# First layer of a hybrid decoder: another spacing of the recurrence's matmuls, and convolutions that scale their copy in SBUF

## The chip, the cores and the metric

The kernel runs on one core of a Trainium2 chip. The metric is the device time of one execution in microseconds (us). Three runs of the kernel before took 2169.34, 2174.07 and 2175.66 us (median 2174.07). The profile that is read below is of one further execution, which took 2167.99 us; its span from the first to the last instruction is 2166.2 us.

## The reference, cut to what matters

A sequence of 1040 tokens (16 meta tokens and 1024 tokens of input) passes two layers of width 1024. The first is a gated DeltaNet: q, k and v come from one projection, a causal convolution over 4 tokens and a SiLU; then a linear recurrence over chunks, per head. The second layer (latent attention) is not touched by the change.

```python
qkv, z, b, a = split(h @ w_in)
qkv = silu(causal_depthwise_conv(qkv, conv_w))        # 4 taps
...
def step(state, xs):                                  # one chunk of one head
    v_new = u_c - w_c @ state
    o_c   = qd_c @ state + a_c @ v_new
    state = state * gl_c + kd_c.T @ v_new
```

## The kernel before, in words

**Work of the first layer.** The 16 value heads are handled as 8 groups of 2 (one query/key head each). For each group, columns of the input projection are computed 128 at a time, transposed: 128 channels on the partitions, 1040 tokens along the free axis, in three pieces of 400, 384 and 256 tokens, each in its own PSUM bank (tile `pt`, tag `proj`, 3 banks in all, so one column of 128 channels fills them). The products are made as three fp32r matmuls (high and low halves), 72 matmuls for a column. A column is a query, a key, one of two gates `z` or one of two values `vT`.

**Emptying a column.** For queries, keys and values `conv_ev` does, for each of the three pieces: copy the last 3 tokens of the piece before out of its bank into the front of an SBUF tile `xpad` (L423), copy the piece itself behind them (L424), scale the piece by the fourth tap into the output tile (L427, on ScalarE, read from the bank `pt`), add the other three taps on VectorE (L429, read from `xpad`), and a SiLU by tanh (L431, L432). `xpad` has 3 buffers. The value column's output `vT` is one tile of 1040 tokens with one buffer: the second value column of a group can be written only when the first one's transposes (L632) have read it. The banks of a column are free for the next column when L423, L424 and L427 have read them.

**The recurrence.** `rec_chunk(g, c)` does chunk c (128 tokens) of group g: `ksp`, the key's product with the state `S` (PE); `r` on VectorE (L739); `xps`, the product of the inverse `U` with `r` (PE); its copy `x` (ScalarE, L747); `sps`, the state's update product (PE); the new state (VectorE, L758); `oq`, the output's products (PE); and the output `o` (L772, L773) with its sum of squares (L783). The state of a chunk is needed by `ksp` of the next. `kd` (L727, GpSimd, one buffer) is made at the chunk's start and read by `sps`.

**What sets the order.** `rec_chunk` is a generator. The loop over groups and chunks takes 5 steps of it per chunk, and after each step some steps of side work (`fills(g)`: the projections, convolutions, the triangular inverse of the next group, all of it independent of this chunk), 77 steps per group over 45 slots, so 1.7 per slot. So the place of a `yield` says how much side work stands between two parts of a chunk. This order of the program text gives each instruction its priority only: a planner orders each engine's queue when the kernel is built. It lets an instruction go ahead of one of higher priority that, by the planner's own estimate of durations, isn't ready. The parts under `with first():` (the two state steps on VectorE and the copy `x`) have priority over everything. On the chip each queue runs in that fixed order; an instruction that waits holds up all behind it.

**A lone bank.** Transposes of k, q, v (`tok_stats`, `v_tokens`) and of the gated outputs (`out_`) share one PSUM bank (tag `tr`). The recurrence's products share four banks (tag `tp`).

Of the kernel before, what the change touches and what calls it, by code (L numbers as in the profile page):

```python
# [9 lines left out]
AF = mybir.ActivationFunctionType  # L10
# [35 lines left out]
def build(nc, tc, A, out, dbg=None):  # L46
    dbg = dbg or {}
    act, dve, pool, pe, sp = nc.scalar, nc.vector, nc.gpsimd, nc.tensor, nc.sync
# [13 lines left out]
    def mm(out_, l, r, start, stop):  # L62
        pe.matmul(out_, l, r, start=start, stop=stop)  # L63
# [108 lines left out]
    with contextlib.ExitStack() as g_es:  # L172
# [170 lines left out]
        @contextlib.contextmanager  # L343
        def first():

            tc.cur_priority -= 4000
            yield
            tc.cur_priority += 4000
# [64 lines left out]
        def conv_ev(ct, dst, new):  # L413

            wc = lambda i: wcv[:, i * 32 + ct:i * 32 + ct + 1]

            def ev(pts, i, n0, n):
                xp = gp.tile([P, 403], F32, name="xpad", bufs=3)
                if i == 0:
                    pool.memset(xp[:, 0:3], 0.0)  # L420
                else:
                    pn = NCH[i - 1][1]
                    act.copy(xp[:, 0:3], pts[i - 1][:, pn - 3:pn])  # L423
                act.copy(xp[:, 3:3 + n], pts[i][:, :n])  # L424
                o = new(i)
                dst.append(o)
                act.activation(o, pts[i][:, :n], AF.Copy, scale=wc(3))  # L427
                for j in (2, 1, 0):
                    dve.scalar_tensor_tensor(o, xp[:, j:j + n], wc(j), o, op0=ALU.mult, op1=ALU.add)  # L429
                t = gp.tile([P, 400], F32, name="tanh", bufs=3)  # L430
                act.activation(t[:, :n], o, AF.Tanh)  # L431
                dve.scalar_tensor_tensor(o, t[:, :n], 1.0, o, op0=ALU.add, op1=ALU.mult)  # L432
            return ev
# [4 lines left out]
        def chunk(src, c):  # L438

            i = [c in cs for _, _, cs in NCH].index(True)  # L440
            t0, n = TOK[c]
            return src[i][:, t0 - NCH[i][0]:t0 - NCH[i][0] + n]
# [277 lines left out]
        def rec_chunk(g, c):  # L720
            s = st[g]
            t0, n = TOK[c]
            kT, qT, AT = s["k"], s["q"], s["AT"][c]
            U = s["U"].pop(c)
            hd = lambda x, h: x[:, c, 2 * g + h:2 * g + h + 1]
            kd = gp.tile([P, 2, 128], F32, name="kd", bufs=1)
            pool.tensor_tensor(kd, s["ktok"][c].unsqueeze(1).broadcast_to([P, 2, 128]),  # L727
                               s["kds"][:, c].unsqueeze(2).broadcast_to([P, 2, 128]), op=ALU.mult)
            if c == 0:
                rr = [s["v"][0, h] for h in range(2)]  # L730
            else:
                S = s["S"]
                ksp = ps.tile([P, 2, 128], F32, name="ksp", tag="tp", bufs=4)
                mm(ksp, chunk(kT, c), S, True, True)
                yield
                r = gp.tile([P, 2, 128], F32, name="r", bufs=1)
                with first():
                    for h in range(2):
                        dve.scalar_tensor_tensor(r[:, h], ksp[:, h], hd(egc, h), s["v"][c, h], op0=ALU.mult, op1=ALU.subtract)  # L739
                rr = [r[:, h] for h in range(2)]  # L740
            xps = ps.tile([P, 2, 128], F32, name="xps", tag="tp", bufs=4)
            for h in range(2):
                mm(xps[:, h], U[:, h], rr[h], True, True)
            yield
            x = gp.tile([P, 2, 128], F32, name="x", bufs=1)
            with first():
                act.copy(x, xps)  # L747
            sps = ps.tile([P, 2, 128], F32, name="sps", tag="tp", bufs=4)
            for h in range(2):
                mm(sps[:, h], kd[:, h], x[:, h], True, True)  # L750
            yield
            Sn = gp.tile([P, 2, 128], F32, name="S", bufs=2)
            if c == 0:
                act.copy(Sn, sps)
            else:
                with first():
                    for h in range(2):
                        dve.scalar_tensor_tensor(Sn[:, h], S[:, h], egl[:, c, 2 * g + h:2 * g + h + 1], sps[:, h],  # L758
                                                 op0=ALU.mult, op1=ALU.subtract)
            s["S"] = Sn  # L760
            oq = ps.tile([P, 2, 2, 128], F32, name="oq", tag="tp", bufs=4)
            for h in range(2):
                mm(oq[:, 1, h], AT[:, h], x[:, h], True, True)
            if c:
                mm(oq[:, 0], chunk(qT, c), S, True, True)
            yield
            o = gp.tile([P, 2, 128], F32, name="o", bufs=8)
            if c == 0:
                act.copy(o, oq[:, 1])
            else:  # L770
                for h in range(2):
                    act.activation(o[:, h], oq[:, 0, h], AF.Copy, scale=hd(egc, h))  # L772
                dve.tensor_tensor(o, o, oq[:, 1], op=ALU.subtract)  # L773
            ci = [c in cs for _, _, cs in NCH].index(True)
            i = NCH[ci][2].index(c)
            if i == 0:
                s["oss"] = gp.tile([P, 4, 2], F32, name="oss", bufs=3)
                s["o"] = []
                if c == 0:
                    pool.memset(s["oss"], 1.0)  # L780
            for h in range(2):
                jk = gp.tile([P, 128], F32, name="jk", bufs=1)
                act.activation(jk[:n], o[:n, h], AF.Square, accum_out=s["oss"][:n, i, h:h + 1])  # L783
            s["o"].append(o)
            if c == NCH[ci][2][-1]:
                gate(g, ci, s["o"], s["oss"])
# [126 lines left out]
        for g in range(8):  # L913
# [5 lines left out]
            for c in range(9):  # L919
                tg = iter(())  # L920
                if c == 0 and g < 2:
                    tg = t_half(g, 0)
                elif c == 1:
                    t_load(g, 1)
                elif c == 3:
                    tg = t_half(g, 1)
                elif c == 7 and 0 < g < 7 or c == 8 and g == 0:
                    st[g + 1]["U"] = {}
                    t_load(g + 1, 0)
                elif c == 8 and g < 7:  # L930
                    tg = t_half(g + 1, 0)
                tg = shifted(tg, TPRIO)
                rg = shifted(rec_chunk(g, c), RPRIO)
                for _ in range(STAGES):
                    next(tg, None)
                    next(rg, None)
                    stages += 1
                    while done * 9 * STAGES < stages * nfill:
                        next(fl_, None)
                        tick()  # L940
                        done += 1
                assert next(tg, None) is None and next(rg, None) is None
# [6 lines left out]
    def bank(tag, bufs):  # L949
        return ps.tile([P, 512], F32, name="b_" + tag, tag=tag, bufs=bufs)  # L950
# [129 lines left out]
    with w1_es:  # L1080
# [62 lines left out]
        for tis in GROUPS:  # L1143
# [3 lines left out]
            pts = [bank("a", 4) for _ in tis]  # L1147
# [481 lines left out]
    with tp_(name="w2", bufs=1) as w2p:  # L1629
# [34 lines left out]
        for tis in groups2:  # L1664
            first = tis[0] == 1
            pts = w2pts if first else [[bank(*(("tr", 3) if ti in (3, 6) else ("a", 4))) for _ in range(2)] for ti in tis]
# [42 lines left out]
```

## Time and profile before

| | us |
|---|---|
| median of three runs | 2174.07 |
| profiled execution | 2167.99 |
| its span | 2166.2 |
| TensorE busy | 2045.9 (94%) |
| VectorE busy | 1359.4 (63%) |
| ScalarE busy | 1102.3 (51%) |
| GpSimd busy | 740.5 (34%) |
| mean granted TensorE clock | 0.980 of full |

The first layer's recurrence lies from about 175 to 1055 us of the span; the groups follow each other about every 118 us. A line of the profile names source line, engine, operation and tiles (out<-in), then its time; a bracket at its end gives how long the engine stood idle before it and what ended the idle time. "Busy" of TensorE counts instructions at whatever clock was granted. The granted clock has two levels, 1.2 and 2.4 GHz; a mean of 0.89 over a stretch is a mixture of both.

### The profile page before, as it was taken

What the parts mean: (1) busy time and instruction counts of PE and PEld (TensorE: products, weight loads), DVE (VectorE), ACT (ScalarE), POOL (GpSimd) and SP (SyncE); (2) the same over time, 40 slices, a digit from 0 to 9 for tenths busy, and PEclk for the clock granted to TensorE, in tenths of its full rate; (3) what the DMA queues carried; (4) which work ended last, traced back from release to release, by engine and by line L of the source; (5) the groups of instructions that cost most, each with busy time, mean ns of one, the idle gap of its engine ahead of it and who ended that gap; (6) DMA issues with size and microseconds to landing.
All of it is one profiled execution on the core that took longest, in us unless ns stands there. A gap on an engine that the chain in (4) does not pass through costs nothing.

```text
span 2166.2 us, 38604 instructions
## 1 busy us (share of the span) xinstructions
PE 2045.9 (94%) x13407; PEld 1823.8 (84%) x13407; DVE 1359.4 (63%) x3135; ACT 1102.3 (51%) x3323; POOL 740.5 (34%) x1718
## 2 busy tenths in 40 slices
PE   7899888999999898999899999999999999999998
PEld 6898778989899898987677898888998999987886
DVE  6585866685858585765446543436777877885422
ACT  5655455656464746555334454335665656664311
POOL 4343535455464545441301482301304132010111
PEclk9999999999999999999899999999999999999999
DMA  3123122222221212124445431221111111124431
GB/s 119 51 55 75 40 61 67 56 66 53 61 62 43 75 51 74 47 66 110 138 116 174 141 91 61 88 95 44 40 50 40 49 35 50 40 81 163 160 100 41
DMA packets 237420, 164.02 MB, mean 76 GB/s; under 512 B 78476, under 2 KB 217304, under 8 KB 237224
## 3 DMA queue, kind: packets, MB, share of 16 engines
q1 hardware_dynamic: 225472, 140.12, 23.0%
q0 software_dynamic: 4128, 13.15, 1.6%
q10 hardware_dynamic: 7624, 8.27, 1.2%
q8 instruction: 106, 1.74, 0.3%
q14 instruction: 90, 0.74, 0.1%
HBM read 121.27 MB, written 40.19 MB: 75 GB/s over the span
## 4 chain that ended last, share of the span: by engine, by line
PE 71%; DVE 15%; DMA 4%; ACT 4%; issue 3%; POOL 2%; SPq 1%; DVEq 0%; ACTq 0%; POOLq 0%
PE b_a L63 27%; PE pt L63 17%; PE b_tr L63 8%; PE b_pv L63 5%; PE b_tr L1493 3%; DVE pr L577 2%; PE oq L63 2%; DVE pr L600 1%; DVE tu L579 1%; PE sps L63 1%; DVE pr L593 1%; DVE MT L549 1%; PE xps L63 1%; DVE AT L550 1%; PE ksp L63 1%
## 5 line engine op out<-in xcount | busy, mean ns | idle before, releaser
L63 PE MATMUL pt<-hsh,whi 128*128 128x400 f32 (+2 forms) x1128 | 372.7, 333 | 14.5 <-ACT xpad L423 10.6
L63 PE MATMUL pt<-hsl,whi 128*128 128x400 f32 (+2 forms) x1128 | 369.6, 328 | 0.0
L63 PE MATMUL pt<-hsh,wlo 128*128 128x400 f32 (+2 forms) x1128 | 368.0, 328 | 1.1 <-POOL wlo L392 1.1
L392 POOL TENSOR_TENSOR wlo<-raw,whi 128x256 fp32r<-128x256 f32 x188 | 154.2, 825 | 252.1 <-ACT whi L391 242.5
L63 PEld LDWEIGHTS pt<-hsh,whi 128*128 128x128 f32 x1128 | 214.5, 190 | 19.6 <-ACT xpad L423 12.4
L63 PEld LDWEIGHTS pt<-hsh,wlo 128*128 128x128 f32 x1128 | 213.3, 190 | 2.9 <-POOL wlo L392 1.8
L63 PEld LDWEIGHTS pt<-hsl,whi 128*128 128x128 f32 x1128 | 214.3, 190 | 1.4
L1469 POOL COPY p<-p 128x32 f32<-128x32 f32 x128 | 28.9, 226 | 334.1 <-ACT p L1466 313.9
L1466 ACT ACTIVATE p<-b_a,mx 128x256 f32<-128x256 f32 (+4 forms) x224 | 120.8, 546 | 41.1 <-DVE mx L1458 17.7
L60 DVE TENSOR_TENSOR ptl<-b_tr,pth 128x512 fp32r<-128x512 f32 x192 | 104.6, 550 | 24.0 <-ACT pth L59 21.8
L59 ACT CAST pth<-b_tr 128x512 fp32r<-128x512 f32 x192 | 91.5, 487 | 51.8 <-PE b_tr L1493 50.3
L1451 DVE TENSOR_REDUCE mx<-b_a 128x1 f32<-128x256 f32 (+4 forms) x224 | 110.9, 504 | 9.0 <-PE b_a L63 5.7
L59 ACT CAST gh<-graw 128x512 fp32r<-128x512 f32 (+1 forms) x86 | 51.0, 602 | 124.8 <-PE b_a L63 83.8
L429 DVE SCALAR_TENSOR_TENSOR vT<-xpad,wcv,vT 128x256 f32<-128x256 f32 (+2 forms) x144 | 92.4, 684 | 30.0 <-ACT xpad L423 25.5
L60 DVE TENSOR_TENSOR gl<-graw,gh 128x512 fp32r<-128x512 f32 x82 | 55.7, 688 | 81.3 <-ACT gh L59 80.0
L391 ACT CAST whi<-raw 128x256 fp32r<-128x256 f32 x188 | 75.5, 404 | 57.0 <-PE pt L63 27.2
L1493 PE MATMUL b_tr<-cm,p 128*128 128x128 f32 x576 | 93.7, 274 | 1.3 <-ACT wt L1373 0.7
L63 PE MATMUL b_a<-hsh,gh 128*128 128x512 f32 (+1 forms) x224 | 87.9, 399 | 5.9 <-ACT ojunk L978 4.2
L1292 DVE SCALAR_TENSOR_TENSOR wlo<-raw,vecs,whi 128x128 fp32r<-128x128 f32 x128 | 45.1, 383 | 72.6 <-ACT whi L1291 70.7
L727 POOL TENSOR_TENSOR kd<-ktok,kds 128x256 f32<-128x256 f32 x72 | 60.7, 843 | 83.9 <-PE sps L63 83.7
L63 PE MATMUL b_a<-hsl,gh 128*128 128x512 f32 (+1 forms) x224 | 87.7, 399 | 0.2
L63 PE MATMUL b_a<-ckth,qah 128*128 128x256 f32 (+4 forms) x224 | 81.8, 365 | 3.9 <-ACT p L1466 3.9
(610 smaller groups left out, 6055.4 us busy)
## 6 DMA issues: line engine op xcount, KB each, us to landing
raw<-in_gdn_w_in SPq DMA_DIRECT2D x192, 128.0 KB, 2.2
graw<-g1scr SPq DMA_DIRECT2D x52, 256.0 KB, 3.3
raw<-in_mla_w_in SPq DMA_DIRECT2D x64, 128.0 KB, 2.2
zscr<-z SPq DMA_DIRECT2D x16, 512.0 KB, 2.8
zh<-zscr SPq DMA_DIRECT2D x32, 256.0 KB, 3.5
g2scr<-g2t POOLq DMA_DIRECT2D x32, 256.0 KB, 3.4
graw<-g2scr SPq DMA_DIRECT2D x30, 256.0 KB, 3.0
wraw<-in_mla_w_out SPq DMA_DIRECT2D x13, 512.0 KB, 4.8
```

The costliest lines, as they stand in the source:

```text
L59: act.copy(hi, src)
L60: dve.tensor_tensor(lo, src, f(hi), op=ALU.subtract)
L63: pe.matmul(out_, l, r, start=start, stop=stop)
L391: act.copy(hi, raw)
L392: pool.tensor_tensor(lo, raw, f(hi), op=ALU.subtract)
L429: dve.scalar_tensor_tensor(o, xp[:, j:j + n], wc(j), o, op0=ALU.mult, op1=ALU.add)
L577: dve.tensor_tensor(prv, T[:, :, 0:i, 0:i].rearrange("p h j c -> p h c j"), bd[:, :, 0:i, i].unsqueeze(2).broadcast_to([65, 2, i, i]), op= ...
L727: pool.tensor_tensor(kd, s["ktok"][c].unsqueeze(1).broadcast_to([P, 2, 128]), s["kds"][:, c].unsqueeze(2).broadcast_to([P, 2, 128]), op=AL ...
L1292: dve.scalar_tensor_tensor(lo[:, i], raw[:, i], gk, f(hi[:, i]), op0=ALU.mult, op1=ALU.subtract)
L1451: dve.tensor_reduce(mx[:, i:i + 1], o, axis=AX.X, op=ALU.max, negate=(m == 1))
L1466: act.activation(p[:, bd[i]:bd[i + 1]], pts[i][:, :n], AF.Exp, bias=nm, accum_out=rsum[:, i:i + 1])
L1493: pe.transpose(tp[:kn, i * 128:(i + 1) * 128], ps4[i][:, 32 + kt0:32 + kt0 + kn], ident)
```

## The change

The convolution's scale step reads the copy in `xpad` instead of the PSUM bank. In the recurrence, one `yield` is added between `r` and `xps`, the one between `sps` and the new state moves behind the new state, and the one between `oq` and `o` is taken out. Counted in the chunk's five steps, `ksp` stays in step 1 and `o` in step 5; `xps` moves from step 2 to 3, `sps` from 3 to 4, `oq` from 4 to 5. Chunk 0 has neither `ksp` nor the new `yield`: its `o` moves from step 4 to 3.

```diff
@@ conv_ev
-                act.activation(o, pts[i][:, :n], AF.Copy, scale=wc(3))
+                act.activation(o, xp[:, 3:3 + n], AF.Copy, scale=wc(3))
@@ rec_chunk
                 rr = [r[:, h] for h in range(2)]
+                yield
             xps = ps.tile([P, 2, 128], F32, name="xps", tag="tp", bufs=4)
...
                 mm(sps[:, h], kd[:, h], x[:, h], True, True)
-            yield
             Sn = gp.tile([P, 2, 128], F32, name="S", bufs=2)
...
                                                  op0=ALU.mult, op1=ALU.subtract)
+            yield
             s["S"] = Sn
             oq = ps.tile([P, 2, 2, 128], F32, name="oq", tag="tp", bufs=4)
...
                 mm(oq[:, 0], chunk(qT, c), S, True, True)
-            yield
             o = gp.tile([P, 2, 128], F32, name="o", bufs=8)
```

## Rows read from the trace of the kernel before

**Rows 1.** The page, part 1: busy time, share of the span, instructions.

```profile
PE 2045.9 (94%) x13407; PEld 1823.8 (84%) x13407; DVE 1359.4 (63%) x3135; ACT 1102.3 (51%) x3323; POOL 740.5 (34%) x1718
```

**Rows 2.** Windows over seven groups: length, busy per engine, PEclk, DMA share, GB/s.

```profile
217.00:975.00 758.00, 700.41 (x5578) 657.01 (x5577) 537.61 (x1200) 422.22 (x1445) 381.87 (x777) 0.96 0.23 59
```

**Rows 3.** Waits of PE in the same stretch: total us, times, longest.

```profile
PE xps L63 <- DVE r L739: 16.4, 12, 2.7
PE pt L63 <- ACT xpad L423: 9.4, 6, 2.3
PE sps L63 <- ACT x L747: 4.4, 9, 1.1
PE tp L814 <- ACT vt L635: 3.6, 6, 0.8
PE kk L63 <- DVE S L758: 2.7, 5, 0.6
```

**Rows 4.** PE's timeline about 590 us: start, us, instruction, count, idle before.

```profile
585.28 0.28 PE L63 MATMUL pt<-hsh,wlo 128*128 128x256 f32 x1
586.71 0.74 PE L63 MATMUL xps<-r,u 128*128 128x128 f32 x4 [1.15 <-DVE r L739]
589.41 0.78 PE L632 MATMUL tp<-cm,vT 128*128 128x128 f32 x4 [1.95 <-DVE gt__7602 L816]
...
591.34 1.06 PE L63 MATMUL oq<-x,AT 128*128 128x128 f32 x4
...
595.94 0.45 PE L63 MATMUL pt<-hsh,whi 128*128 128x400 f32 x1
```

**Rows 5.** ACT's timeline in the same gap.

```profile
585.30 0.86 ACT L424 COPY xpad<-pt 128x400 f32<-128x400 f32 x2
...
595.22 0.61 ACT L427 ACTIVATE vT<-pt,wcv 128x400 f32<-128x400 f32 x1
595.70 0.19 ACT L423 COPY xpad<-pt 128x3 f32<-128x3 f32 x1
...
596.25 0.44 ACT L424 COPY xpad<-pt 128x256 f32<-128x256 f32 x1
```

**Rows 6.** Windows about each such gap, columns as in rows 2.

```profile
92.00:106.00 14.00, 9.94 (x54) 8.91 (x53) 6.99 (x25) 9.13 (x36) 6.46 (x21) 0.76 0.16 39
184.00:200.00 16.00, 12.76 (x94) 11.55 (x95) 10.78 (x38) 12.41 (x51) 2.39 (x5) 1.00 0.07 18
212.00:236.00 24.00, 18.84 (x159) 15.42 (x158) 20.66 (x54) 8.54 (x28) 8.56 (x22) 0.86 0.04 12
...
345.00:363.00 18.00, 13.61 (x68) 11.97 (x67) 12.37 (x26) 11.04 (x38) 5.21 (x9) 0.81 0.35 83
467.00:483.00 16.00, 12.30 (x65) 10.61 (x64) 11.19 (x19) 10.78 (x39) 6.23 (x10) 0.89 0.45 123
585.00:600.00 15.00, 11.24 (x59) 9.69 (x59) 10.56 (x18) 10.23 (x35) 5.79 (x8) 0.89 0.43 120
703.50:718.50 15.00, 11.03 (x59) 9.51 (x58) 10.27 (x18) 10.27 (x36) 6.04 (x9) 0.89 0.47 122
820.50:835.50 15.00, 11.22 (x59) 9.71 (x58) 10.54 (x19) 9.85 (x34) 5.64 (x7) 0.89 0.42 120
938.00:954.00 16.00, 12.10 (x61) 10.74 (x60) 10.78 (x21) 8.91 (x30) 3.50 (x8) 0.79 0.33 89
```

**Rows 7.** ACT's groups by shape: busy us, mean ns, idle before and its releasers.

```profile
L772 ACT ACTIVATE o<-oq,egc 128x128 f32<-128x128 f32 x128 | 39.7, 361 | 45.5 <-PE oq L63 45.5
...
L431 ACT ACTIVATE tanh<-vT 128x400 f32<-128x400 f32 x16 | 8.6, 538 | 34.6 <-DVE vT L429 34.6
...
L650 ACT ACTIVATE tanh<-pt 128x400 f32<-128x400 f32 x16 | 7.9, 497 | 3.5 <-PE pt L63 3.5
```

**Rows 8.** PE's row at the next stop of that group.

```profile
616.46 0.45 PE L63 MATMUL pt<-hsh,whi 128*128 128x400 f32 x1 [1.98 <-ACT xpad L423]
```

**Rows 9.** ACT's timeline ahead of that stop.

```profile
614.26 0.40 ACT L543 ACTIVATE AT<-gcb,ngct 128x128 f32<-128x128 f32 x1 [2.87 <-POOL gcb L536]
```

## Prediction

> **What bounds the kernel now.** I read the page first: TensorE is busy 94% of the span, the other three far less [rows 1], so time can go only where TensorE stands idle or runs at its lower clock. Next the windows over the seven groups of the first layer, since both edits lie there: of 758 us TensorE is busy 700.4, so 57.6 us are idle, and at a mean granted clock of 0.96 another 758 x 0.04 = 30 us of work are lost [rows 2]. Idle time and clock are one matter here: most windows with a gap show 0.76 to 0.89 where the stretch as a whole shows 0.96 [rows 2, 6]. Third, the waits of TensorE, which name the releasers: `r` of VectorE 16.4 us, the 3-token copy L423 9.4, the copy `x` 4.4, then transposes [rows 3].
>
> That list undersells one cause. In the timeline about 590 us the last projection matmul of a value column starts at 585.28 and the next column's first at 595.94. Between them TensorE does only recurrence products and transposes, and each wait is booked to its own releaser (1.15 on `r`, 1.95 on the gate's product) [rows 4]. What is missing in these 10.7 us is projection work to put between. ScalarE shows why: it copied two pieces into `xpad` at 585.30, and then neither the first scaling L427 nor the 3-token copies L423 ran until 595.22 and 595.70; TensorE starts right behind [rows 4, 5]. L427 writes `vT`, which has one buffer, and must wait until the first value column has been transposed. L423 of the second piece only reads the first piece's bank and writes `xpad`; yet it comes after L427, and the second piece's copy L424, which reads another bank, came ten microseconds before it. So I read the order as a tie between the two reads of one bank: the copy stands behind the scaling that has nowhere to write. The same picture recurs in every group: the windows of rows 6 hold it in eight places (the third window has another cause, below).
>
> **The change part by part.**
>
> *The scaling from SBUF.* L427 no longer touches the bank. L423 and L424 then need only `xpad`, three buffers for three pieces, so the banks should be free at about 586 to 587 us instead of 595.7, and the next column, 72 matmuls, can fill the gap. What that is worth, per window of rows 6: idle = length minus busy, clock loss = length x (1 - PEclk). 92: 4.06 + 3.36 = 7.4; 184: 3.24 + 0 = 3.2; 345: 4.39 + 3.42 = 7.8; 467: 3.70 + 1.76 = 5.5; 585: 3.76 + 1.65 = 5.4; 703: 3.97 + 1.65 = 5.6; 820: 3.78 + 1.65 = 5.4; 938: 3.90 + 3.36 = 7.3. Sum 47.6 us [rows 6]. All of it is the upper bound. The lower bound supposes that the named waits stay, since `gt` and the copies of `vt` are as late as before and TensorE's queue can't pass them: of the 3.76 us of the fifth window, 1.95 is on `gt` [rows 4], and if the clock still falls only the rest, 1.8 us of 5.4, comes back: a third, 16 us over the eight. I take 60%, between the ends and somewhat to the upper one, because a queue with projection work between these waits meets most of them late enough: 47.6 x 0.6 = 28.6 us. The window 212 to 236 I leave out (8.5 us [rows 6]): there the blocked tile is a key's, held by the recurrence's own chunks, and the work pulled ahead is soon held by the same tile; bounds 0 and 8.5.
>
> *What it costs.* Read from SBUF instead of PSUM a 400-token activation takes 538 ns against 497 (tanh of L431 and of L650) [rows 7]. I take 41 ns for each of the 96 scalings: 3.9 us of ScalarE, beside 336 us that ScalarE is idle in the stretch [rows 2]. The scaling must now see the finished copy; nothing of before shows that pair. If it cost a whole 41 ns more 32 times on TensorE's path (once per column) that is 1.3 us; if L423 instead goes ahead of L427 in every column, it gives back up to the 0.48 us that L427 takes between its start and L423's [rows 5], 15 us if all 32 stood on the path. But six waits on L423 in the stretch sum to 9.4 us [rows 3] and some are made by something else: the one at 616.46 follows a ScalarE queue that stood 2.87 us behind GpSimd's mask [rows 8, 9], which the change doesn't touch. I take 0, bounds -1.3 and +3.
>
> A rule speaks against this edit: the Trainium skill, Perfetto Trace Analysis, "Optimizing Scalar/DVE Operations", gives ScalarE an access overhead of about 93 ns on SBUF and 51 ns on PSUM. The trace's 41 ns agrees. By the rule the 96 scalings would cost 4.0 us of ScalarE, and the sum stays as it is.
>
> *Two slots between `ksp` and `xps`.* The side work of one more slot (the windows of rows 6 follow each other by about 118 us, over 45 slots 2.6 us) stands between `r` and the product that needs it. Waits on `r` are at most 2.7 us [rows 3], so by itself the slot all but covers them. Of the 16.4 us some 10 lie inside the eight windows, one wait in each from 345 on (1.15 us in the fifth [rows 4]), and are counted there; 6.4 lie elsewhere. VectorE is 71% busy in the stretch [rows 2], and what it is late with will in part turn up as another wait: I take 2.5 us of 6.4. Bounds 0 and 6.4.
>
> *Two slots for the state.* The path from `sps` to the next `ksp` has one slot less. `kk` waits for the state's step 2.7 us now [rows 3]; with the cover of a slot gone it could double. Since the state step has priority over all of VectorE's work in either version, I take 1 us of loss, bounds 0 and 2.7. `kd` of the next chunk waits for `sps` on GpSimd and comes one slot later; behind it stand low halves of weights, and it is used three slots on: 0.
>
> *`oq` and `o` in one slot.* L772 already stands 45.5 us on `oq` over 128 instructions [rows 7]; ScalarE has the idle time for more, but what is queued behind it are the copies that free banks. I take 0 here; its price is the rival below.
>
> Sum against the profiled execution: 28.6 + 0 + 2.5 - 1 = 30 us, 2168 to 2138. The median of the runs shown is 6 us above the profiled one; on that scale 2144. I say 2143.
>
> The Trainium skill, Perfetto Trace Analysis, "Identifying Performance Opportunities", says that the same gap, repeated on the engine that should be saturated, can mean that there is no SBUF or PSUM for the next tile. Rows 4 to 6 agree, but the rule points at two cures, more banks or another buffer for `vT`; releasing the banks earlier is the first of them. Were `vT` the place that binds, the rule's gain wouldn't come, which is the second rival.
>
> **The rivals.** Times on the runs' scale.
>
> 1. *The gap is filled and given back.* TensorE reaches the next things that VectorE and GpSimd are late with (the `gt` at 589.41, the mask's chain at 614.26) that much earlier and stands there longer. For it: the longest wait in the gap is on VectorE, not on a bank [rows 4], and the stop at 616 is GpSimd's doing [rows 8, 9]. Against it: over the seven groups VectorE is busy 71% and GpSimd 50% of the time, TensorE 92% [rows 2], so what they are late with in one place they make up in another. Then only clock and small waits come back, a quarter of 47.6: 2174 - 12 = 2162.
>
> 2. *Nothing to fill it.* The third piece's copy L424 also ran only at 596.25, although its matmuls were done by 585.6 [rows 4, 5]; no bank tie explains that. If what holds it (an `xpad` or an order on the queue) holds the others too, the banks stay shut as before. The recurrence's spacing alone then gives 1.5 us: 2172.
>
> 3. *Slower: ScalarE blocked by the outputs.* With no slot between `oq` and `o`, L772 comes to the head of ScalarE's queue before `oq` has run. The first four matmuls of an `oq` took 1.06 us in the gap [rows 4], so 64 chunks add up to at most 68 us of ScalarE standing still, to the 45.5 of now [rows 7]. The waits of TensorE that ScalarE ends (9.4 + 4.4 + 3.6 = 17.4 us [rows 3]) double and drag the clock with them, while the filled gaps give half of what I count, because the freeing copies stand behind L772: +17.4 +8 - 14 = +11, 2185. It decides from where the copies L423 run more than 2 us after their column's last matmul in most columns.
>
> **How the numbers follow.** My forecast 0.58, rival 1 0.19, rival 2 0.11, rival 3 0.12. The forecast's own range is 2120 (all 47.6 and the 6.4) to 2158 (a third of it). The range for 8 in 10 takes in rival 1 and rival 2 and some of the 8.5 us left out: 2116 to 2175; outside are rival 3 and a thin lower tail. A difference under 0.3% (6.5 us) can't be told from none: faster is the forecast and nearly all of rival 1, 0.75; same is rival 2 and a little of rival 1, 0.13; slower is rival 3, 0.12.
>
> **What would show it.** In the changed profile L423 and all L424 of a second value column should run within 2 us of the column's last matmul, with L427 some 8 us later; the gap in `pt` matmuls should fall from 10.7 us to under 3; the windows of rows 6 should show clocks above 0.95; waits on `r` should be under 8 us. If banks are released early and TensorE's idle time in the same seven groups is still above 50 us, rival 1 holds; if L423 still follows L427 ten microseconds late, rival 2; if L772's idle time passes 80 us, rival 3. A median above 2167.5 would make the forecast wrong.

## The result, and the profile after

The changed kernel is slower: 2204.27 us (median of 4, 2198.07 to 2210.59) against 2172.78, ratio 1.0146 [1.0113, 1.0179]. The forecast of 2143 was wrong in size and in sign. The profiled execution took 2203.37 us, 35.4 more than that of before.

First the windows over the same seven groups; they end 34 us later now. Columns as in [rows 2].

```profile
217.00:1009.00 792.00, 708.61 (x5578) 661.24 (x5577) 550.58 (x1207) 426.95 (x1445) 386.19 (x778) 0.95 0.22 56
```

It is the same 5578 products, in 792 us instead of 758. TensorE's idle time went from 57.6 to 83.4 us, and its busy time for the same products from 700.4 to 708.6, at a mean granted clock of 0.95 instead of 0.96: 25.8 and 8.2 make up the 34 us.

TensorE's waits in that stretch (total us, times, longest), to set beside [rows 3]:

```profile
PE ksp L63 <- DVE S L758: 22.8, 9, 5.2
PE tp L814 <- ACT vt L635: 9.8, 4, 3.5
...
PE sps L63 <- ACT x L748: 6.3, 7, 2.6
PE xps L63 <- DVE r L739: 5.6, 5, 2.4
```

The wait on `r` fell from 16.4 to 5.6 us and that on L423, 9.4 before, is down to 0.8. In their place stand the state `S` (1.2 us before) and `vt` (3.6). How they came about, timelines of one second value column on three engines show. ScalarE first (start, us, instruction, count, idle before it):

```profile
720.39 0.49 ACT L424 COPY xpad<-pt 128x400 f32<-128x400 f32 x1 [0.78 <-PE pt L63]
720.78 0.17 ACT L423 COPY xpad<-pt 128x3 f32<-128x3 f32 x1
...
724.63 0.47 ACT L424 COPY xpad<-pt 128x384 f32<-128x384 f32 x1
725.00 0.15 ACT L423 COPY xpad<-pt 128x3 f32<-128x3 f32 x1
...
727.17 0.36 ACT L424 COPY xpad<-pt 128x256 f32<-128x256 f32 x1
...
730.12 1.12 ACT L635 ACTIVATE vt<-tp,rki 128x128 f32<-128x128 f32 x4
...
736.65 0.51 ACT L543 ACTIVATE AT<-gcb,ngct 128x16 f32<-128x16 f32 x2 [4.81 <-POOL gcb L532]
...
739.69 1.11 ACT L635 ACTIVATE vt<-tp,rki 128x128 f32<-128x128 f32 x4
740.69 1.54 ACT L427 ACTIVATE vT<-xpad,wcv 128x400 f32<-128x400 f32 x3
```

The banks are released long before the scaling, as intended: no copy waits for a scaling any more. (The third copy still starts 4.2 us after the column's last product ended at 722.99, where the prediction wanted 2, since ScalarE waited for VectorE ahead of it.) But the scaling, ten us behind the column's first copy before [rows 5], is twenty behind it now: ScalarE's queue runs in order, and at its head stand the mask's exponentials L543, waiting for GpSimd's `gcb`. VectorE has nothing to tap meanwhile:

```profile
741.41 5.58 DVE L429 SCALAR_TENSOR_TENSOR vT<-xpad,wcv,vT 128x400 f32<-128x400 f32 x8 [10.09 <-ACT vT L427]
...
747.85 0.60 DVE L758 SCALAR_TENSOR_TENSOR S<-S,egl,sps 128x128 f32<-128x128 f32 x2
```

Then eight taps come at once, and the state's update stands in VectorE's queue behind them. TensorE stops for both:

```profile
740.85 1.12 PE L814 MATMUL tp<-cm,o 128*128 128x128 f32 x4 [3.47 <-ACT vt L635]
...
748.60 1.19 PE L63 MATMUL ksp<-S,k 128*128 128x256 f32 x2 [3.90 <-DVE S L758]
```

### The profile page after: what moved, and what is told of

The parts are those of the page before. It is cut to its first block, busy times and chain, and to the rows that moved or that the text cites. A ratio compares the mean times of both kernels' runs of the same rounds, so it can differ in the third digit from the quotient of the medians.

```text
span 2201.5 us, 38692 instructions
## 1 busy us (share of the span) xinstructions
PE 2054.4 (93%) x13407; PEld 1828.3 (83%) x13407; DVE 1370.2 (62%) x3135; ACT 1107.0 (50%) x3323; POOL 745.4 (34%) x1718
## 4 chain that ended last, share of the span: by engine, by line
PE 65%; DVE 16%; DMA 6%; POOL 5%; ACT 3%; issue 3%; SPq 1%; DVEq 0%; POOLq 0%; ACTq 0%
PE b_a L63 27%; PE pt L63 13%; PE b_tr L63 8%; PE b_pv L63 5%; DVE vT L429 3%; PE b_tr L1493 3%; DVE pr L577 2%; DVE pr L600 1%; PE oq L63 1%; DVE tu L579 1%; DVE MT L549 1%; DVE pr L593 1%; PE sps L63 1%; DVE AT L550 1%; DMA bm<-mscr 1%
## 5 line engine op out<-in xcount | busy, mean ns | idle before, releaser
L63 PE MATMUL pt<-hsh,whi 128*128 128x400 f32 (+2 forms) x1128 | 379.6, 338 | 9.2 <-DVE zs L651 6.8
L392 POOL TENSOR_TENSOR wlo<-raw,whi 128x256 fp32r<-128x256 f32 x188 | 161.4, 863 | 237.5 <-ACT whi L391 224.2
L429 DVE SCALAR_TENSOR_TENSOR vT<-xpad,wcv,vT 128x400 f32<-128x400 f32 (+2 forms) x144 | 89.0, 662 | 55.7 <-ACT vT L427 55.5
L1451 DVE TENSOR_REDUCE mx<-b_a 128x1 f32<-128x256 f32 (+4 forms) x224 | 110.9, 504 | 10.5 <-PE b_a L63 7.0
L727 POOL TENSOR_TENSOR kd<-ktok,kds 128x256 f32<-128x256 f32 x72 | 52.4, 728 | 99.6 <-PE sps L63 99.4
```

Of the source, the lines that this page charges most:

```text
L392: pool.tensor_tensor(lo, raw, f(hi), op=ALU.subtract)
L1451: dve.tensor_reduce(mx[:, i:i + 1], o, axis=AX.X, op=ALU.max, negate=(m == 1))
```

## The experiments: the scaling from SBUF

Every ratio below is to the kernel before, run beside it. In kernels with lines added or dropped the line numbers of the rows shift by one or two. The change was first cut in two. **e1** has only the convolution's edit:

```diff
-                act.activation(o, pts[i][:, :n], AF.Copy, scale=wc(3))
+                act.activation(o, xp[:, 3:3 + n], AF.Copy, scale=wc(3))
```

> Only the scaling reads the SBUF copy; the recurrence's spacing is that of before. Theory A (the early release itself does the harm: TensorE's queue gets the next column's matmuls ahead of the value transposes, the value column is written some 20 us after its copies instead of 10, and VectorE stands idle there): most of the loss is here, 2190 to 2205 us, VectorE idle for 8 us or more ahead of the second value column's taps in each group. Theory B (the spacing does the harm: with a slot less between the update product and the next state product, TensorE waits on the state, 22.8 us in the changed kernel against 1.2): this one is as fast as before or faster, 2140 to 2175, and its waits of ksp on the state stay under 5 us.

Measured: 1.0069 [1.0048, 1.0091]. **e2** is the changed kernel with that line put back, so it has only the spacing:

```diff
-                act.activation(o, xp[:, 3:3 + n], AF.Copy, scale=wc(3))
+                act.activation(o, pts[i][:, :n], AF.Copy, scale=wc(3))
```

> Only the recurrence's spacing is changed; the scaling reads PSUM as before. Theory A: within 8 us of before (2165 to 2181), waits of ksp on the state under 6 us. Theory B: 2190 to 2205, with waits of ksp on the state near the 22.8 us of the changed kernel, and waits of xps on r under 8 us.

Measured: 1.0060 [1.0042, 1.0079]. Each half costs some 14 us and the halves nearly add up (1.29% of 1.46%); neither theory had both. In e1 one stop comes back from group to group, six waits of `sps` on `x` that sum to 22.2 us. Of GpSimd, ScalarE and TensorE there (start, us, instruction, idle before it):

```profile
737.34 2.51 POOL L536 TENSOR_TENSOR gcb<-gcb,cm 128x384 f32<-128x384 f32 x2 [3.80 <-DMA gcb<-gcscr]
```

```profile
738.74 0.98 ACT L543 ACTIVATE AT<-gcb,ngct 128x128 f32<-128x128 f32 x3 [2.69 <-POOL gcb L536]
739.88 0.98 ACT L543 ACTIVATE AT<-gcb,ngct 128x128 f32<-128x128 f32 x3
...
741.20 0.35 ACT L747 COPY x<-xps 128x256 f32<-128x256 f32 x1
```

```profile
741.69 1.19 PE L63 MATMUL sps<-x,kd 128*128 128x128 f32 x4 [4.38 <-ACT x L747]
```

Read upwards: TensorE waits for `x`, which stands in ScalarE's queue behind exponentials that wait for GpSimd, which waits for a DMA into `gcb`. That tile's one place is shared with `pr` of the triangular inverse, so by the code the DMA can't start while the inverse uses it. Three kernels give `gcb` its own place; an unused constant mask is dropped to make the room:

```diff
-                gcb = gp.tile([P, 2, 400], F32, name="gcb", bufs=1)
+                gcb = gp.tile([P, 2, 400], F32, name="gcb", tag="gcm", bufs=1)
```

**e3**, this in the changed kernel:

> The changed kernel with a buffer of its own for the decay mask's rows (gcb), which it shared with the inverse's products; an unused 128-column constant is dropped to make room. The rows can then be loaded and masked before the inverse is done, so ScalarE's exponentials L543 no longer stand 4.8 us at the head of its queue with the value copies L635 and the scaling L427 behind them. Theory C (ScalarE held by the mask is what makes the value column late): half or more of the loss is gone, 2175 to 2190, and the wait of L543 on GpSimd falls by more than half. Theories A and B: within 8 us of the changed kernel, less the control's own gain.

Measured: 1.0084 [1.0052, 1.0115], 0.6% of the change's 1.46% comes back. The wait of the exponentials on `gcb` falls from 45.2 us over the whole span to 13.6, more than by half as theory C wanted; the time that comes back is a little less than its half. **e4**, this in the kernel before:

> Control for the run with the mask's own buffer: the same buffer in the kernel before. Theory C: little to gain, 2160 to 2174, since there the exponentials stand behind the value copies; the 2 us stop of TensorE about 616 us should go in each group, up to 10 us in all. Theories A and B say nothing of it.

Measured: 1.0018 [1.0006, 1.0030]. **e6**, this in e1:

> The scaling from SBUF alone, spacing as before, and the mask's staging tile gcb in a place of its own (an unused constant mask dropped for the room). Theory C (with the scaling from SBUF TensorE comes earlier to where ScalarE's queue stands on the mask's exponentials, and x, vt and the scaling stand behind them): the wait of sps on x, 24 us with the scaling alone, falls below 8 us and the time to 2160 to 2175. Theory A (the pulled work itself costs, the mask is only where it shows): 2180 to 2190 as without the buffer, the wait turning up elsewhere.

Measured: 0.9988 [0.9973, 1.0003]. So the staging place is what the scaling's half lost through: 1.0069 - 0.9988 = 0.81%, 17.6 us. The same place gives the old kernel nothing; it costs it 0.18%. The wait of `sps` on `x` is 4.0 us in e6. Theory C holds for the scaling. **e12** scales from SBUF only in the value columns:

```diff
-                act.activation(o, pts[i][:, :n], AF.Copy, scale=wc(3))
+                act.activation(o, xp[:, 3:3 + n] if ct >= 16 else pts[i][:, :n], AF.Copy, scale=wc(3))
```

> The scaling from SBUF for the value columns alone; key and query columns are still scaled from the bank, and spacing and mask are as before. Theory A/C (the loss of the scaling alone, +0.69%, comes from the value column's gap being filled): 2182 to 2190, with sps waiting some 20 us on x behind the mask's exponentials. Theory H (it comes from the key and query columns' order or from the dearer read): 2165 to 2176.

Measured: 1.0096 [1.0070, 1.0122]: the loss is the value columns', the place of the gap.

**Where the gain went.** In e6 the gap about the value column is broken up, and the exponentials' wait on `gcb` is down to 16.5 us over the whole span, from 57.0 in e1. Still there is little to see of 28.6 us. The windows of e6 over the same seven groups, columns as in [rows 2]:

```profile
217.00:973.00 756.00, 695.44 (x5635) 650.38 (x5634) 557.43 (x1213) 423.38 (x1441) 380.74 (x774) 0.98 0.23 59
```

TensorE's idle time is 60.6 us, not less than the 57.6 of before; what little was gained is the clock, 0.98 against 0.96. TensorE's timeline of e6 at the start of a group:

```profile
526.61 0.28 PE L62 MATMUL pt<-hsh,wlo 128*128 128x256 f32 x1
526.73 0.49 PE L813 MATMUL tp<-cm,o 128*128 128x128 f32 x3
...
539.90 0.79 PE L62 MATMUL sps<-x,kd 128*128 128x128 f32 x4
540.44 0.43 PE L62 MATMUL pt<-hsh,whi 128*128 128x400 f32 x1
```

and the same place of the kernel before:

```profile
531.37 0.28 PE L63 MATMUL pt<-hsh,wlo 128*128 128x256 f32 x1
531.49 0.60 PE L452 MATMUL tp<-cm,q 128*128 128x128 f32 x4
...
538.98 0.45 PE L63 MATMUL pt<-hsh,whi 128*128 128x400 f32 x1
```

There is a second stretch without projections in each group, at its start, when all three banks hold the first `z` column. Measured from the end of one `pt` product to the start of the next, it was 7.3 us and is 13.6. In the four groups from about 400 us on, e6 has 11.5 to 13.6 us at the start and 2.3 to 4.5 at the value column (two pieces), where before had 7.3 to 7.7 and 10.4 to 10.6. All stretches over 2 us without projections sum to 22 to 25 us a group before, 23 to 26 in e6 and 29 to 36 in the changed kernel. The projections that fill one gap are missing in the next.

**e5** closes the gap by the other way, two buffers for `vT` with the scaling from the bank (the unused mask dropped, `AT` with 15 places instead of 16):

```diff
-                vT = gp.tile([P, L], F32, name="vT", bufs=1)
+                vT = gp.tile([P, L], F32, name="vT", bufs=2)
...
```

> The kernel before (scaling from the bank, spacing as before) with two buffers for vT instead of one; to make room in SBUF an unused constant mask is dropped and AT has 15 places instead of 16. The scaling of a second value column then needn't wait for the transposes of the first, and the banks come free though it still reads them. Theory D (the gap of some ten us in the projection matmuls was worth little: what is filled there is given back at the next thing that VectorE, GpSimd or ScalarE is late with): 2160 to 2185, TensorE's idle time over the seven groups falls by less than 10 us or rises. Theory E (the gap is worth what it holds, and the change's edit lost it since value columns were still scaled, tapped and transposed late): 2125 to 2155, idle time falls by 15 us or more.

Measured: 1.0180 [1.0156, 1.0204], 2206.38 us. Theory E falls; D had the direction and missed the size. The start gap is 11 to 14 us here too, all stretches without projections sum to 27 to 32 us a group, and TensorE's costliest wait is on GpSimd's scaling of `o`, 12.7 us against 1.0 before. What the place that `AT` lost costs was not run by itself, so the loss is not shown to be the buffer's alone. **e9** tries to shorten the start gap in e6 by asking for each group's last outputs earlier, since these release `zs`:

```diff
-                later(OUT7 if g == 7 else OUTL, lambda: out_(0), False)
+                later(OUT7 if g == 7 else 8 if ci == 2 else OUTL, lambda: out_(0), False)
-            later(SC7 if g == 7 else SCL, scale, False)
+            later(SC7 if g == 7 else 5 if ci == 2 else SCL, scale, False)
```

> The scaling from SBUF with the mask's own staging tile and the old spacing (2166 us, no gain over before), and in it the output of each group's last piece of tokens asked for earlier (scaled 5 instead of 9 side slots after the gate, transposed 8 instead of 14 slots after that). Theory F (what was pulled into the value column's gap is missing at the group's start, where the three banks hold the first z column until the previous group's last outputs free zs): the gap in projection matmuls at the group's start falls from 11.5 to 13.6 us to under 9 us and the time to 2145 to 2160. Theory G (at the group's start the projections wait for something else, or the gap moves on once more): the gap stays above 10 us or turns up elsewhere, 2163 to 2175.

Measured: 1.0148 [1.0118, 1.0178]. F's numbers fall, the start gap stays at 12 to 15 us; G's too, since 1.6% was lost against e6. TensorE's costliest wait there:

```profile
PE tp L813 <- POOL o L802: 22.6, 24, 3.6
```

But e9 didn't bring the outputs earlier. Of before, e6 and e9, two rows each: the first of the two output products that release `zs` (VectorE), and the tanh that empties the `z` column's first bank (ScalarE):

```profile
533.47 0.46 DVE L816 SCALAR_TENSOR_TENSOR gt__6909<-tp,onh,zs 128x256 f32<-128x256 f32 x1
536.58 0.86 ACT L650 ACTIVATE tanh<-pt 128x400 f32<-128x400 f32 x2
```

```profile
534.49 0.46 DVE L815 SCALAR_TENSOR_TENSOR gt__6909<-tp,onh,zs 128x256 f32<-128x256 f32 x1
537.58 0.86 ACT L649 ACTIVATE tanh<-pt 128x400 f32<-128x400 f32 x2
```

```profile
538.93 0.48 DVE L815 SCALAR_TENSOR_TENSOR gt__6670<-tp,onh,zs 128x256 f32<-128x256 f32 x1 [3.01 <-PE tp L813]
541.18 0.89 ACT L649 ACTIVATE tanh<-pt 128x400 f32<-128x400 f32 x2 [0.83 <-DMA g1scr<-gt__6670]
```

In five groups the tanh comes 2.2 to 3.4 us behind that product in all three kernels. Counted from the end of the `z` column's last product, the output product comes after 1.8 to 2.3 us before, 5.3 to 8.2 in e6 and 7.5 to 10.5 in e9. So in e6 the column comes earlier and its release doesn't, as F had it, while e9 moved the release the wrong way. What a shorter start gap would give is not shown.

## The experiments: the spacing

**e7** adds the slot for `r` and takes the state's, with `oq` and `o` still apart; **e8** only moves the state's `yield`; **e16** only joins `oq` and `o`; **e10** adds the slot for `r` and a sixth slot to the chunk, so that nothing is taken:

```diff
e7                 rr = [r[:, h] for h in range(2)]
+                yield
...
                 mm(sps[:, h], kd[:, h], x[:, h], True, True)
-            yield
e8             (the same yield after sps removed)
+            yield
             s["S"] = Sn
e16                mm(oq[:, 0], chunk(qT, c), S, True, True)
-            yield
e10                rr = [r[:, h] for h in range(2)]
+                yield
-        MRATE, BRATE, NFILL, N0, STAGES, N7 = 1.0, 1.2, 77, 86, 5, 64
+        MRATE, BRATE, NFILL, N0, STAGES, N7 = 1.0, 1.2, 77, 86, 6, 64
```

> The kernel before with the slot between r and xps added and the one between sps and the state's update taken away; oq and o stay in two slots (the change also joins these). Theory B1 (what harms in the spacing is oq and o in one slot): 2168 to 2176. Theory B2 (what harms is the shorter way from x to the next ksp, which both have): 2179 to 2187, with the wait of ksp on S above 8 us. Theory B3 (any new spacing upsets orders that fit the old one): also 2179 or more, but with no more than 4 us of ksp on S.

> The kernel before with the slot between sps and the state's update moved to behind the update: the update is issued one slot earlier, so that two slots instead of one lie between it and the next ksp; no slot is added before xps, and oq and o stay in two slots. Theory B1 and B2 alike: 2165 to 2175, waits on r as before (some 18 us), ksp on S under 2 us. Theory B3 (any new spacing upsets orders that fit the old one): 2179 or more.

> The kernel before with oq and o in one slot and no other change: the fifth slot of a chunk then holds only side work. Theory B2: 2165 to 2176, what ScalarE stands on oq may grow but TensorE's waits don't. Rival (the third one of the prediction: outputs at the head of ScalarE's queue hold the copies that free banks): 2178 or more, with the stops of TensorE on ScalarE's copies L423 and x doubled.

> The kernel before with six slots in a chunk instead of five: a slot is added between r and xps and none is taken away; the same side work is spread over six slots. Theory B2 (the spacing harms because r's slot was taken from the way x, state, next ksp): 2160 to 2174, gaps in projection matmuls at the value column no longer than before (10.4 us). Theory B4 (in a gap that has no projections, every further stop in the chunk's chain is one more wait that nothing fills, wherever the slot came from): 2179 to 2190, the value column's gap 11.5 to 14 us and the one at the group's start 10 us or more, as with the change's spacing alone.

Measured, with TensorE's waits on the three links of the chain over the seven groups (us): of `xps` on `r`, of `sps` on `x` and of `ksp` on `S`.

| | ratio | `r` | `x` | `S` | sum |
|---|---|---|---|---|---|
| before | 1 | 16.4 | 4.4 | 1.2 | 22.0 |
| e8 | 1.0008 [0.9994, 1.0022] | 12.8 | 4.9 | 1.0 | 18.7 |
| e10 | 1.0017 [1.0003, 1.0031] | 2.7 | 15.2 | 6.3 | 24.2 |
| e2 | 1.0060 [1.0042, 1.0079] | 8.5 | 9.5 | 9.3 | 27.3 |
| e16 | 1.0066 [1.0042, 1.0090] | 10.6 | 18.6 | 2.4 | 31.6 |
| e7 | 1.0098 [1.0075, 1.0121] | 5.5 | 15.8 | 3.9 | 25.2 |
| after | 1.0146 [1.0113, 1.0179] | 5.6 | 6.3 | 22.8 | 34.7 |

For instance these rows of e7 and of e10:

```profile
PE sps L63 <- ACT x L748: 15.8, 9, 2.7
...
PE xps L63 <- DVE r L739: 5.5, 6, 1.4
```

```profile
PE sps L63 <- ACT x L748: 15.2, 8, 2.5
...
PE xps L63 <- DVE r L739: 2.7, 4, 1.1
```

Every version with a slot behind `r` waits less on `r` (2.7 to 8.5 us), and the time stands at the links further down. Only e8 has a smaller sum than before, and it gains nothing. In e7 `sps` is two slots before the next `ksp`; in e10 it is three again, and 0.8% come back. B1 (the joining is what harms) fell with e7. B3 (any new spacing harms) fitted e7, with 3.9 us on `S` where B2 wanted over 8, and fell with e8. B2 fitted e10, and B4 fell there. And e16, where B2 failed, shows that the joining by itself costs as much as the whole spacing: the pieces don't add.

Two places through which the spacing could have cost were taken away. First `kd`'s single buffer, on which GpSimd stands 129 us in the first 1000 us of e7 (65 before):

```diff
-            kd = gp.tile([P, 2, 128], F32, name="kd", bufs=1)
+            kd = gp.tile([P, 2, 128], F32, name="kd", bufs=2)
```

In e7 (**e13**), in the kernel before (**e14**) and in the changed one (**e15**):

> The slot for r alone (+0.98%), with two buffers for kd instead of one. There GpSimd stands 129 us on sps before it may write the next chunk's kd (65 us in the kernel before). Theory K (the spacing harms through kd: sps comes nearer to the next chunk, and the low halves, masks and output scalings queued behind kd come late): 2168 to 2178. Theory B2 (it harms on the way x, state, next ksp itself, and kd is only late beside it): 2183 to 2192, waits of sps on x still above 10 us.

> The kernel before with two buffers for kd and nothing else. Theory K: as fast as before or up to 10 us faster, 2160 to 2172. Theory B2: 2165 to 2176, no gain, since in the old spacing nothing that TensorE waits for stands behind kd for long (1.1 us on low halves, 1.0 us on output scalings).

> The changed kernel (2204 us) with two buffers for kd. Theory K: 2185 to 2195, half of the spacing's part and some of the mask's come back. Theory B2: 2198 to 2208.

Measured: 1.0069 [1.0052, 1.0086], 0.9993 [0.9981, 1.0004] and 1.0168 [1.0152, 1.0184]: `kd` has no part in before and in the changed kernel; the 0.3% by which e13 lies under e7 is within the intervals. Second, the mask. In e16 ScalarE and TensorE show the stop of e1 again:

```profile
740.38 0.99 ACT L543 ACTIVATE AT<-gcb,ngct 128x128 f32<-128x128 f32 x3 [5.68 <-POOL gcb L536]
```

```profile
743.36 0.90 PE L632 MATMUL tp<-cm,vT 128*128 128x128 f32 x3 [3.46 <-ACT vt L635]
```

**e17** is e16, **e18** is e2, each with `gcb` in its own place:

> oq and o in one slot as the only change of the spacing (+0.66%), with the mask's staging tile in a place of its own (an unused constant mask dropped for the room). Theory M (what the joined outputs cost is again ScalarE standing at the mask's exponentials: 43 us on GpSimd's gcb against 28 in the kernel before, once a group 5.7 us with vt behind it and TensorE stopped 3.5 us): 2168 to 2178. Rival N (any new order of the recurrence costs some 12 us, the mask is only where it is seen): 2181 to 2190, with the waits on x still 15 us or more.

> The change's whole spacing with the scaling from the bank as before, and the mask's staging tile in a place of its own. Theory M can't say much here, since ScalarE stands no longer on gcb than in the kernel before (28 against 33 us): 2175 to 2184. Rival N: 2178 to 2190, no gain from the buffer; the gaps in projection matmuls stay 11 us or more at both places.

Measured: 1.0084 [1.0052, 1.0115] and 1.0086 [1.0053, 1.0118]. Theory M falls. The stop shown is gone in e17, and another has its place (24.0 us on GpSimd's `o`, 1.0 before):

```profile
PE tp L812 <- POOL o L801: 24.0, 22, 3.6
```

N was right in time and wrong in what it foresaw: the wait on `x` is 1.5 us in e17, and in e18 the value column's gap is 8.8 to 14.9 us, not always over 11. As a rule for any new order it had already fallen, with e8 and e10. Last, **e11**, six slots on e6:

> The same six slots on top of the scaling from SBUF with the mask's own staging tile (2166 us without them). Theory B2: 2155 to 2168. Theory B4: at least 2173, though less is lost than on the kernel before because the value column's gap is filled here.

Measured: 1.0069 [1.0047, 1.0091], the time of B4, with 24.2 us on `S`; but B4 foresaw less loss than in e10, and what costs 0.17% there costs 0.8% on e6. B2 falls here (it wanted 2155 to 2168, measured 2182), so none of the theories fits all versions.

## Why the prediction was wrong, step by step

**The scaling from SBUF** (28.6 us) is the step that failed. The first part of its mechanism came: the banks open before the scaling, the wait on L423 is 0.8 us, rival 2 is refuted, and in e6 the gap is broken into two of 2.3 to 4.5 us. The 60% failed. Its reason, that projections between the waits let TensorE meet them late enough, supposed more projections; there are only those that the next gap then lacks, and e6's idle time is 60.6 us where before had 57.6. (The 47.6 us were also a little high: they count the clock loss over whole windows, idle time included; over busy time alone the windows of [rows 6] give 43.) By the test set for rival 1 (banks released early and idle time over 50 us) rival 1 holds, at 83.4 us, though the kernel before would have met the 50 too. Its mechanism is what e6 shows, priced too high: a gain of 12 us was given and 0.12% or 2.6 us [loss 0.7, gain 5.9] measured against before, 0.3% against its like e4.

**What the edit doesn't touch** was the second error. The stop behind the mask at 616 us [rows 8, 9] was left out of the sum as GpSimd's doing, which the change doesn't touch; only rival 1 named that chain. TensorE, running earlier, met it unfinished, with `x`, `vt` and the scaling behind it: 17.6 us, the difference of e1 and e6.

**The dearer read** was over-priced but harmless. Over all 96 scalings L427 took 54.9 us before and 56.3 after, 15 ns each more, not 41.

**The slot for `r`.** The wait on `r` fell by 10.8 us in the changed kernel, more than the whole 6.4 that lay outside the gaps; the price of 2.5 took no account of the loop of five slots, in which that slot was another link's.

**The state's lost slot** (1 us, bounds 0 and 2.7) is the worst-sized term: TensorE's wait on `S` went from 1.2 to 22.8 us, beyond its bound. In e2, where at most single taps stand in front of the state, it is 9.3. In the changed kernel five of the nine waits, 17.3 us of the 22.8, come right behind such taps: the two edits together. The mask is not all of what puts them there, since with its own place (e3) the wait is still 17.2 us. The priority of the state's step was no cover: it stands in one fixed queue behind taps.

**`oq` and `o` in one slot** was priced 0 and costs 0.66% alone. Rival 3 had the sign, but its way isn't borne out: L423 held TensorE 9.8 us in e16 against 9.4, only `x` rose, to 18.6, and when that was taken away in e17 (1.5) no time came back. The output's scaling (L772 of before) stood idle 53.0 us there against 45.5, 72.4 in the changed kernel, under the 80 that it named. **`kd`** at 0 was right.

On the skill: its rule on consistent bubbles (Trainium skill, Perfetto Trace Analysis, "Identifying Performance Opportunities") was taken as two cures, banks or a buffer. Both were tried, e6 and e5; the gap at the value column shrank, but e6's time can't be told from before's and e5 lost 1.8%: the stretches without projections came back elsewhere. The 93 against 51 ns for ScalarE on SBUF and PSUM (Trainium skill, Perfetto Trace Analysis, "Optimizing Scalar/DVE Operations") differ by 42 ns, as the tanh of 400 columns does by 41 [rows 7]; this scaling differs by 15.

**Open:** why e2, e16 and e7 cost 13, 14 and 21 us while e8 costs nothing and e10 4. Neither the mask's place nor `kd` explains it. The chain's waits don't give the size (e10 and e7 differ by 1.0 us in their sums and by 0.8% in time), nor do the stretches without projections (27 to 31 us a group in e10, 27 to 33 in e2). The stops appear at another engine each time; whether the planner's new order of the queues does it, rather than the slots, no run separates. No version tried beat the kernel before measurably.

## What to carry to other kernels

A gap on the busiest engine is worth its length only if there is work that isn't needed to fill the next gap; add up all stretches without filler over a period before pricing one. The sum tells whether a gap was closed or moved; e10 shows that it isn't a price. In a loop with a fixed number of slots, a slot given to one link is another link's. And when an edit lets one engine run ahead, price what it will meet, the shared buffers and in-order queues that the edit doesn't touch.

## What the runs showed of the hardware

A scaling of 400 columns on ScalarE took 601 ns from PSUM (mean of 32 before) and 629 from SBUF (mean of 32 after), one of 256 columns 508 and 509: the difference that the tanh shows, 41 ns at 400, is not the same for every operation and length. And a stop can cost twice: behind the stops of 3.47 and 3.90 us the mean granted clock of a stretch in which TensorE was busy throughout was 0.51, nearly all of it at the lower of its two levels (1.2 GHz); then it was 1.00 again (windows of the changed kernel, columns as in [rows 2]):

```profile
749.00:754.00 5.00, 5.00 (x16) 4.78 (x16) 4.96 (x11) 3.70 (x13) 0.55 (x2) 0.51 0.50 134
754.00:760.00 6.00, 6.00 (x43) 5.93 (x42) 1.98 (x4) 2.21 (x7) 5.21 (x15) 1.00 0.02 4
```
